# A Fourier mixer on one Trainium2 core: the transform along the features moves from the data to the projection's weights

## The chip, the cores and the metric

One core of a Trainium2 chip runs the whole program. The metric is device time in microseconds (us), from one launch to its end. Engines are called as the profile calls them: PE (matrix multiplies), DVE (vector), ACT (activations, casts), POOL (GpSimd), SP (issues most DMAs). All numbers are fp32; a matmul operand is split in a high part that PE multiplies exactly and a low rest, and a product takes three matmuls (high·high, high·low, low·high).

## The reference

Two sequences, s (512 tokens) and p (1,024 tokens), of 1,024 features go through two layers. The first layer's mixer is the subject:

```python
def fourier_mixer(x, g, w):
    b, s, d = x.shape
    h = rms_norm(x, g).astype(jnp.float32).reshape(b, s, N_FGROUPS, FGROUP_DIM)   # 8 groups of 128
    mixed = jnp.real(jnp.fft.fft2(h, axes=(1, 3), norm="ortho"))
    return mixed.reshape(b, s, d).astype(x.dtype) @ w

# layer 0: x = x + fourier_mixer(x, norm_mix[0], fourier_w)
# layer 1: x = x + attention_mixer(...)
# after each: x = x + (silu(h @ w_gate) * (h @ w_up)) @ w_down     with h = rms_norm(x, norm_ffn[i])
```

The real part of the two-dimensional transform is (cosine along tokens)·(cosine along features) minus (sine)·(sine). All of it is linear, so the transform along the features can be applied to `h` or, transposed, to the rows of `w`.

## The kernel before, in words

Tokens are handled in blocks of 512 columns: one for s, two for p. The program runs in this order.

1. The mixer of s (`lead()`, which runs `mixer("s")`), alone. Rows of tokens are loaded (`load_rows`), squared and summed on ACT (`stats_rows`), and `rsqrt` makes the row scales `r_s` on DVE. Rows are folded along the tokens (`combine`: ACT scales, DVE adds, ACT and DVE split). For each of the 8 feature groups, PE multiplies by the token cosines and sines `mat_s` (`spectra`; a group costs 15 matmuls of 256 or 258 columns and 3 with the fixed row), ACT and DVE split the result into `sd`, and after two groups `features` multiplies by the feature cosines and sines `dd`. Its result is split into `eo`. Beside it the projection's weights of columns 0 to 3 are loaded and folded (`folded`: two POOL sums of 512 columns, an ACT cast, a POOL subtraction of 1,024 columns).
2. The projection of s (`mixer_projection("s")`): 8 column blocks n, each 25 matmuls `eo`·`w` of 256 or 258 columns (one of them with `w64`, the rows that the fold leaves over), then four to five DVE additions to the residual `acc` and a sum of squares. Weights 4 to 7 are folded while it runs; four steps of p's mixer are issued ahead of it.
3. The feed-forward of s, `ffn(0, 0)`: 22 chunks `fc`, each of 72 matmuls of 512 columns (gate and up into two PSUM banks `g`; ACT's silu, the product on DVE (L758) and the split `mid`; then down into `c`, added to `acc` on DVE, L728). A weave issues it together with p's mixer and projection (`aux_0`), by estimated costs of both. Here p's `spectra` and `features` run per group on 128x256 pieces. The result goes to DRAM (`du`), and `spectra_back` loads it again and splits it. The projection of p then loads and folds all 8 weights once more (`folded` with tag `wX`), 50 matmuls for each.
4. The other feed-forwards, woven with attention and its projections. The diff does not touch them.

Every engine takes its instructions in the order in which they were placed, and the tile framework's scheduler chose that order; `pinned` keeps a place. Buffers are shared by tag: `g` has two PSUM banks, `c` (F) two, and `a` one pair of banks.

Of the kernel before, what the change touches and what calls it, by code (L numbers as in the profile page):

```python
# [59 lines left out]
def dft_constants():  # L60
# [31 lines left out]
    i = np.arange(P)  # L92
    ang = 2 * np.pi / P * ((i[:, None] * np.arange(64)[None, :]) % P)
    cos, sin = np.cos(ang), np.sin(ang)
    cos[:, 0] = 0.5
    full = np.zeros((5, P, 192))
    full[0, :, 64:128], full[1, :, 64:128] = split_host(cos)
    full[2, :, 64:128], full[3, :, 64:128] = split_host(sin)
    full[4, :, 64] = (-1.0) ** i

    alt = np.zeros((P, 112))
    alt[:, [8, 40, 72]] = full[4, :, 64:65]
    out["dft_d"] = np.concatenate([full.transpose(1, 0, 2).reshape(P, -1), alt], axis=1).astype(np.float32)
# [20 lines left out]
def trunk_kernel(ctx: ExitStack, tc: tile.TileContext, t: dict):  # L124
# [95 lines left out]
    g_mix0, g_mix1 = gains[:, 0:8], gains[:, 8:16]  # L220
    g_ffn = (gains[:, 16:24], gains[:, 24:32])
    g_q, g_k = gains[:, 32:33], gains[:, 33:34]
    rqc = cp.tile([P, 12, NH], F32, name="rqc")
# [3 lines left out]
    du = dram.tile([P, 2, 4, 514], F32, name="du")  # L227
# [75 lines left out]
    def in_rows(y, temp=None):  # L303

        r = bank()
# [72 lines left out]

    def load_rows(seq):
        if seq == "p":  # L380
            x = h_slot("x_p", F32, "A")[:, 0 : 8 * D].rearrange("p (c n) -> p c n", c=8)
            xs = [x[:, c] for c in range(8)]
        else:
            halves = [w_tile2(2, D) for _ in range(2)]
            xs = [halves[c // 2][:, c % 2] for c in range(4)]
# [4 lines left out]
    def stats_rows(seq, n):  # L390
# [3 lines left out]
        xs = whole[seq]  # L394
        for c in range(n):
            raw = raw_tile(D)
            pinned(act.activation(raw, xs[c], AF.Square, accum_out=s[:, c : c + 1]))
        yield 1.0
        rsqrt(r, s, 1.0 / D, bank()[:, 0 : 4 * n])
        return xs, r  # L400
# [8 lines left out]
    def mixer(seq, done):  # L409
# [4 lines left out]
        rows, r = yield from stats_rows(seq, n)  # L414
# [13 lines left out]
        u = None if two else eo_tile(258, "B")  # L428
        r_ps = None if two else tl("c", [TB], F32, "cX", pools["psX"])

        def alternating(o, x):

            for g in range(NC):
                for b in range(2):
                    v = x(g, b)
                    if v is not None:
                        k = 8 - g % 2 * 4 - g // 2
                        pe.matmul(o, alt[:, k : k + 96], v, start=g == 0 and b == 0, stop=g == NC - 1 and b == 1)

        spec = mpt.tile([P, 2, 2, NC, 2], F32R, name=f"spec_{seq}")  # L440
        ncomb = 2 if two else 1

        def half(v, k):
            return v[:, k * 256 : (k + 1) * 256]

        def combine(q, c):

            def x(k):
                return half(rows[k], q)

            comb = w_tile(ncomb, 2, 2, 256) if two else tl("comb", [ncomb, 2, 2, 256], F32R, ("wF", "rawF")[c])
            fa, fb = (bank(), bank()) if two else (lambda v: (v[:, 0], v[:, 1]))(bank2())
            fs = tmp() if two else None
            for i in range(npair):
                ca, cb = 4 * i + c, 4 * i + 2 + c
                dst = fb if i == npair - 1 else fs
                act.activation(half(fa, i), x(ca), AF.Copy, scale=r[:, ca : ca + 1])
                for k, w in enumerate(scal(cb)):
                    ins = dve.scalar_tensor_tensor(half(dst, k), x(cb), w, half(fa, i), op0=ALU.mult, op1=ALU.add)
                    if two and q == 1 and c == 0:  # L460
                        pinned(ins)
            if not two:
                split(comb[:, 0, :, 0], comb[:, 0, :, 1], fb.rearrange("p (k n) -> p k n", k=2))
                return comb
            for k in range(2):
                e = tmp()
                ops = (ALU.add, ALU.subtract)
                dve.tensor_tensor(half(e, 0), half(fs, k), half(fb, k), op=ops[k])
                dve.tensor_tensor(half(e, 1), half(fs, k), half(fb, k), op=ops[1 - k])
                if k == 1 and c == 0:  # L470
                    xb = tmp(256)
                    dve.tensor_scalar(xb[0:1], x(2)[0:1], r[0:1, 2:3], None, op0=ALU.mult)
                    dve.scalar_tensor_tensor(
                        e[0:1, 256:512], x(6)[0:1], neg[0:1, 6:7], xb[0:1], op0=ALU.mult, op1=ALU.add
                    )
                split(comb[:, k, :, 0], comb[:, k, :, 1], e.rearrange("p (k n) -> p k n", k=2), eng=pool)
            return comb

        def fixed_row(q):

            xr = tmp(256)
            if two:
                xb = tmp(256)
# [836 lines left out]
```

## Time and profile before

| | us |
|---|---|
| median of 3 runs | 3119.56 (3114.71 to 3119.58) |
| the profiled execution, its own time | 3117.2 |
| its span in the trace | 3115.4 |
| PE busy | 3024.0 (97%) |
| DVE, ACT, POOL busy | 1630.1, 1240.3, 1334.4 |

The span leaves 1.8 us of the execution's own time outside. PE is busy in 97% of the span, and its granted clock is 0.9 or more in all but the first of 40 slices; a busy PE at half clock still counts as busy, so both must be read together.

### The profile page before, as it was taken

Reading aid. Unit: us, or ns where it says so; the run is one execution under the profiler, and the core shown is the slowest. Engines: PE = TensorE matmul, PEld = TensorE weight load, DVE = VectorE, ACT = ScalarE, POOL = GpSimd, SP = SyncE. Lnnn points to the kernel's source line nnn. Section 1 sums busy time; section 2 is a strip of 40 time slices with the busy share of each in tenths; the row PEclk is TensorE's granted clock in tenths of the full one; section 3 lists DMA queues with packets and bytes.
Section 4 is the critical chain, followed back from the end, with each engine's and each line's share of the span. In section 5 each row is a group of like instructions: output and inputs, shape, how many; then the busy total and the mean of one; then the engine's idle time right before and its main releaser. Section 6 shows DMA issues by size and latency. Waiting matters only on the chain. (4 is left out here: it accounts for less than half of the span.)

```text
span 3115.4 us, 37725 instructions
## 1 busy us (share of the span) xinstructions
PE 3024.0 (97%) x14554; PEld 2492.2 (80%) x14554; DVE 1630.1 (52%) x2888; ACT 1240.3 (40%) x1806; POOL 1334.4 (43%) x624
## 2 busy tenths in 40 slices
PE   8799999999999999999999999999999999999999
PEld 7787888888887778888878788888787787777777
DVE  4763454454366553353455466656337555655556
ACT  5443232333366632233334477767324222222221
POOL 3645454434333454443343322221546644554452
PEclk7999999999999999999999999999999999999999
DMA  5224553333233554343343311211645411111111
GB/s 192 77 79 131 166 180 101 119 105 99 82 90 99 171 169 132 125 132 103 104 150 98 105 58 57 66 60 51 208 139 189 175 54 55 48 54 49 53 48 61
DMA packets 127927, 329.83 MB, mean 106 GB/s; under 512 B 15314, under 2 KB 23506, under 8 KB 127236
## 3 DMA queue, kind: packets, MB, share of 16 engines
q1 hardware_dynamic: 126164, 318.49, 32.1%
q10 hardware_dynamic: 1296, 4.75, 0.4%
q0 software_dynamic: 288, 4.19, 0.4%
q8 instruction: 114, 1.87, 0.2%
q14 instruction: 65, 0.53, 0.1%
HBM read 282.28 MB, written 45.10 MB: 105 GB/s over the span
## 5 line engine op out<-in xcount | busy, mean ns | idle before, releaser
L277 POOL TENSOR_TENSOR w<-raw,w 128x1024 fp32r<-128x1024 f32 x346 | 826.7, 2399 | 1234.2 <-ACT w L276 1200.1
L728 DVE TENSOR_TENSOR acc<-c,acc 128x512 f32<-128x512 f32 x704 | 482.8, 688 | 479.2 <-PE c L247 475.7
L276 ACT CAST w<-raw 128x1024 fp32r<-128x1024 f32 x346 | 362.2, 1048 | 490.3 <-PE c L247 263.4
L245 PE MATMUL g<-h,w 128*128 128x512 f32 x1408 | 555.2, 394 | 1.3 <-ACT h L238 1.1
L246 PE MATMUL g<-h,w 128*128 128x512 f32 x1408 | 551.5, 392 | 0.6 <-POOL h L239 0.6
L247 PE MATMUL g<-h,w 128*128 128x512 f32 x1408 | 551.2, 392 | 0.0
L245 PE MATMUL c<-mid,w 128*128 128x512 f32 x1056 | 417.4, 397 | 11.3 <-DVE acc L728 6.7
L246 PE MATMUL c<-mid,w 128*128 128x512 f32 x1056 | 414.3, 392 | 3.7 <-DVE mid L239 3.7
L247 PE MATMUL c<-mid,w 128*128 128x512 f32 x1056 | 413.7, 392 | 0.0
L239 POOL TENSOR_TENSOR w<-raw,w 128x1024 fp32r<-128x1024 f32 (+1 forms) x101 | 228.2, 2266 | 340.2 <-ACT w L238 319.1
L838 DVE TENSOR_TENSOR acc<-c,acc 128x512 f32<-128x512 f32 x352 | 240.5, 689 | 191.2 <-PE c L247 190.6
L247 PEld LDWEIGHTS g<-h,w 128*128 128x128 f32 x1408 | 265.0, 188 | 54.7 <-POOL w L277 0.3
L245 PEld LDWEIGHTS g<-h,w 128*128 128x128 f32 x1408 | 265.0, 188 | 53.2 <-ACT h L238 1.3
L246 PEld LDWEIGHTS g<-h,w 128*128 128x128 f32 x1408 | 265.1, 188 | 52.8 <-POOL h L239 1.3
L245 PEld LDWEIGHTS c<-mid,w 128*128 128x128 f32 x1056 | 198.1, 188 | 72.7 <-DVE acc L728 16.6
L246 PEld LDWEIGHTS c<-mid,w 128*128 128x128 f32 x1056 | 198.8, 188 | 43.8 <-DVE mid L239 5.7
L247 PEld LDWEIGHTS c<-mid,w 128*128 128x128 f32 x1056 | 198.6, 188 | 40.3
L246 PE MATMUL c<-h,w 128*128 128x512 f32 x480 | 188.1, 392 | 3.2 <-POOL h L239 3.0
L245 PE MATMUL c<-h,w 128*128 128x512 f32 x480 | 189.2, 395 | 0.0
L247 PE MATMUL c<-h,w 128*128 128x512 f32 x480 | 187.0, 390 | 0.0
L238 ACT CAST w<-raw 128x1024 fp32r<-128x1024 f32 (+1 forms) x101 | 100.2, 1000 | 202.1 <-PE a L247 86.6
L1050 DVE TENSOR_REDUCE col<-a 128x1 f32<-128x1024 f32 (+1 forms) x96 | 100.3, 1045 | 129.2 <-PE a L247 128.9
(305 smaller groups left out, 4996.7 us busy)
## 6 DMA issues: line engine op xcount, KB each, us to landing
raw<-in_down_dram SPq DMA_DIRECT2D x110, 512.0 KB, 3.5
raw<-in_gate_dram SPq DMA_DIRECT2D x88, 512.0 KB, 3.5
raw<-in_up_dram SPq DMA_DIRECT2D x88, 512.0 KB, 3.6
raw<-in_qkv_dram SPq DMA_DIRECT2D x36, 512.0 KB, 3.5
t<-xres SPq DMA_DIRECT2D x56, 256.0 KB, 3.9
raw<-in_wo_dram SPq DMA_DIRECT2D x24, 512.0 KB, 3.4
raw<-in_gate_dram SPq DMA_DIRECT2D x44, 256.0 KB, 2.6
raw<-in_up_dram SPq DMA_DIRECT2D x44, 256.0 KB, 2.9
```

The lines of the kernel that those rows point to most:

```text
L238: act.copy(hi, src)
L239: eng.tensor_tensor(lo, src, hi.bitcast(F32), op=ALU.subtract)
L245: pe.matmul(out, lh, rh, start=first, stop=False)
L246: pe.matmul(out, lh, rl, start=False, stop=False)
L247: pe.matmul(out, ll, rh, start=False, stop=last)
L276: pinned(act.copy(flat[:, 0], raw)) if early else act.copy(flat[:, 0], raw)
L277: pool.tensor_tensor(flat[:, 1], raw, flat[:, 0].bitcast(F32), op=ALU.subtract)
L728: dve.tensor_tensor(acc[dc], ps, acc[dc], op=ALU.add)
L838: dve.tensor_tensor(acc, ps, acc, op=ALU.add)
L1050: dve.tensor_reduce(st[:, 0:1], s_in, op=ALU.max, axis=AX.X)
```

## The change

The feature transform and the feature fold move to the weights and to the rows.

- Weights: `turned_weights` loads the 8 pieces of the projection's matrix (64 folded rows of two groups, 512 columns each), sums and subtracts them (DVE and POOL), splits them, multiplies by the feature cosines and sines with PE, and splits the products into `turned` (used by s straight from SBUF). It writes the unsplit products to DRAM (`cwd`), from where p's projection loads them as plain weights. It runs inside s's mixer, one piece for each step.
- Rows: `prepared` multiplies each row chunk by the gain (in PSUM as rows, `in_rows(gx)`) and folds it along the features: four DVE operations of 128x512 for a chunk of 128 tokens (4 chunks in s, 8 in p). `mixer` then transforms along the tokens only, in `along`, for four pairs of groups: half as many matmuls. Results are split straight into `eo` for p also (`spread`). `du` and `spectra_back` are gone.
- Constants come by POOL's DMAs without a staging tile. One step of p's mixer is issued ahead of s's projection instead of four. The weave's cost for p's part is 105 instead of 140 (times `SLACK`).

```diff
-    def stats_rows(seq, n):
+    def prepared(seq, n, ga, gb, sums):
...
+        for c, x in enumerate(whole[seq]):
+            sq = raw_tile(D) if seq == "p" else bank2().rearrange("p k n -> p (k n)")
+            pinned(act.activation(sq, x, AF.Square, accum_out=s[:, c : c + 1]))
+            y = tl("c", [TB], F32, "cX", pools["psX"])
+            f = sums[c]
+            dve.tensor_tensor(f[:, 0], ga, x[:, 0:TB], op=ALU.mult)
+            dve.tensor_tensor(y, gb, x[:, TB:D], op=ALU.mult)
+            dve.tensor_tensor(f[:, 1], f[:, 0], y, op=ALU.subtract)
+            dve.tensor_tensor(f[:, 0], y, f[:, 0], op=ALU.add)
+            yield 1.0
         rsqrt(r, s, 1.0 / D, bank()[:, 0 : 4 * n])
...
+        def along(k, o, lhs, row):
+
+            for (i, off, w), ps in zip(outs[k], o):
+                extra = k == 0 and i == 0
+                for c in range(2):
+                    m = mat[c][:, :, off : off + w]
+                    mm3(ps[:, 0:w], lhs(c, 0, i), lhs(c, 1, i), m[:, 0], m[:, 1], c == 0, c == 1 and not extra)
...
-    def spectra_back(done):
...
+    def turned_weights(w64, dd, odd, alt):
...
+        def operand(n):
+            raw = raws.pop(0)
+            f = tl("f", [2, TB], F32, "rawF")
+            pinned(dve.tensor_tensor(f[:, 0], raw[:, 0], raw[:, 1], op=ALU.add))
+            pool.tensor_tensor(f[:, 1], raw[:, 0], raw[:, 1], op=ALU.subtract)
+            w = acc_tile("wm", [2, 2, TB], F32R)
+            pinned(act.copy(w[:, 0], f))
+            pool.tensor_tensor(w[:, 1], f, w[:, 0].bitcast(F32), op=ALU.subtract)
...
+        def product(n):
...
+            for k in range(2):
+                ps = bankg()
+                mm3(ps, dd[:, 2 * k], dd[:, 2 * k + 1], w[:, 0, k], w[:, 1, k], True, k == 1)
+                if k == 0:
+                    pe.matmul(ps, alt[0:96, j], w64[0:96, h * TB : (h + 1) * TB], start=False, stop=True)
+                    for b in range(2):
+                        pe.matmul(od[0:96], odd[:, 8 - j : 104 - j], w[:, b, 0], start=j == 0 and b == 0, stop=j == 3 and b == 1)
+                split(wt[:, 0, k], wt[:, 1, k], ps)
+                c = tl("t", [TB], F32, "tX")
+                if k == 0:
+                    act.copy(c, ps)
+                else:
+                    dve.tensor_copy(c, ps)
+                sp.dma_start(cwd[h][:, :, k, j, :], c.rearrange("p (n c) -> p n c", n=4))
...
             if two:
-                w, _ = folded(n, "wX")
+                for m in range(len(ws), min(n + 2, NC)):
+                    ws.append(weights(cwd[m // 4][:, m % 4].rearrange("p k j c -> p (k j c)")))
...
     def lead():
-        m = mixer("s", got_s)
+        ws = turned_weights(w64, dd, odd, alt)
+        next(ws)
+        stacked(w64[0:96], stage[0:96], 64)
+        m = mixer("s", got_s, u_s, xrs_s, zz_s)
         for k, v in enumerate(m):
             yield v
...
+            if k in (1, 3) or k >= 5:
+                next(ws, None)
...
-    for _ in range(4):
+    for _ in range(1):
         next(x_0)
     weave(follow(), 1.0)
-    weave(ffn(0, 0, lambda: first["h"]), FFN_US, x_0, (80.0 + 60.0) * SLACK)
+    weave(ffn(0, 0, lambda: first["h"]), FFN_US, x_0, (45.0 + 60.0) * SLACK)
```

The order of instructions shows three places. The first is DVE at the start of s's mixer. Before, `rsqrt` follows at once on the casts of the constants, and its last step, the row scales `r_s`, leads straight to the mask, the fixed row and the first folds; `x_139` holds rows, `m_252` a masked scale.

```order
L291 SCALAR_TENSOR_TENSOR r_s<-c_238,col_239 128x4
L405 TENSOR_TENSOR m_252<-r_s,mask 128x1
L421 TENSOR_SCALAR neg_s<-r_s 128x4
L487 TENSOR_SCALAR t_284<-x_139,r_s 1x256
L406 TENSOR_SCALAR m_252<-m_252 128x1
L487 TENSOR_SCALAR t_382<-x_139,r_s 1x256
L459 SCALAR_TENSOR_TENSOR a_261<-x_139,m_252,a_261 128x256
L239 TENSOR_TENSOR xrs_286<-t_284,xrs_286 1x256
L459 SCALAR_TENSOR_TENSOR a_261<-x_139,m_252,a_261 128x256
```

In the changed kernel these stand ahead of `rsqrt` (`x_140`, `x_141` are the rows, `x_249`, `x_250` the folded sums, `c_159` and `c_172` the gain, `stage_152` the leftover rows of the weights, `f_267` a folded piece of them).

```order
L406 TENSOR_TENSOR x_250<-c_159,x_141 128x512
L407 TENSOR_TENSOR c_255<-c_172,x_140 128x512
L611 TENSOR_TENSOR eo_150<-stage_152,eo_150 32x1024
L408 TENSOR_TENSOR x_249<-x_249,c_255 128x512
L407 TENSOR_TENSOR c_262<-c_172,x_140 128x512
L409 TENSOR_TENSOR x_249<-c_255,x_249 128x512
L408 TENSOR_TENSOR x_249<-x_249,c_262 128x512
L407 TENSOR_TENSOR c_277<-c_172,x_141 128x512
L409 TENSOR_TENSOR x_249<-c_262,x_249 128x512
L631 TENSOR_TENSOR f_267<-raw_243 128x512
L408 TENSOR_TENSOR x_250<-x_250,c_277 128x512
```

So 16 operations of `prepared`, the split L611 and two folds L631 stand where none stood; two splits of the first turned weight (L241 of `w_326`) stand around the end of `rsqrt`, and the row scales come after the first of them.

The second place is DVE at the start of `ffn(0, 0)`. Before, the product with silu for chunk 0 (L758, on `g_1213`) comes after the last row of `normed` (L345), p's splits and three folds of 128x256:

```order
L345 SCALAR_TENSOR_TENSOR t_1208<-acc_788,gains,c_1166 128x512
L242 SCALAR_TENSOR_TENSOR sd_1234<-a_1236,gains,sd_1234 128x2x128 x2
L242 SCALAR_TENSOR_TENSOR spec_p<-a_1236,gains,spec_p 128x2
L242 SCALAR_TENSOR_TENSOR sd_1235<-a_1258,gains,sd_1235 128x2x128 x2
L242 SCALAR_TENSOR_TENSOR spec_p<-a_1258,gains,spec_p 128x2
L459 SCALAR_TENSOR_TENSOR t_1316<-x_p_690,m_735,c_1314 128x256 x2
L459 SCALAR_TENSOR_TENSOR c_1315<-x_p_690,m_738,c_1314 128x256
L758 TENSOR_TENSOR g_1213<-g_1213,t_1419 128x512
```

In the changed kernel, 25 operations of `prepared` for p (L406 to L409) stand between the last row of `normed` (now L347) and the same product, now L785 on `g_1093`. The last two of them and what follows, up to the split of `mid_1224`:

```order
L409 TENSOR_TENSOR x_p_682<-c_1209,x_p_682 128x512
L407 TENSOR_TENSOR c_1216<-a_1109,x_p_682 128x512
L785 TENSOR_TENSOR g_1093<-g_1093,t_1221 128x512
L408 TENSOR_TENSOR x_p_682<-x_p_682,c_1216 128x512
L406 TENSOR_TENSOR x_p_682<-a_1109,x_p_682 128x512
L409 TENSOR_TENSOR x_p_682<-c_1216,x_p_682 128x512
L241 TENSOR_TENSOR mid_1224<-g_1093,mid_1224 128x512
```

So the split of chunk 0's `mid` is the 30th operation behind the last L347; before it came after few and shorter ones.

The third place is PE at the same point in the changed kernel. After chunk 0's gate and up (48 matmuls into the two banks of `g_1093`) come chunk 1's gate into `g_1242` (24) and its up into `g_1243`, which takes the bank that `mid_1224` has to be read from first; here is the end of that and the first `c<-mid` of chunk 0:

```order
L248 MATMUL g_1243<-h_1059,w_1234 128x512
L249 MATMUL g_1243<-h_1059,w_1234 128x512
L247 MATMUL g_1243<-h_1059,w_1234 128x512
L248 MATMUL g_1243<-h_1059,w_1234 128x512
L247 MATMUL c_1283<-mid_1224,w_962 128x512
L247 MATMUL c_1315<-mid_1224,w_962 128x512
L249 MATMUL g_1243<-h_1059,w_1234 128x512
L248 MATMUL c_1283<-mid_1224,w_962 128x512
L249 MATMUL c_1283<-mid_1224,w_962 128x512
```

No matmul of p stands ahead of or among these rows after the start of `ffn(0, 0)`, where before p's `a<-mat_p` did; in the changed kernel p's first one stands some 300 rows later.

## Rows read from the trace of the kernel before

**Rows 1.** Of the profile's page, its parts 1 and 2: busy time by engine; then PE's granted clock in 40 slices of the span.

```profile
PE 3024.0 (97%) x14554; PEld 2492.2 (80%) x14554; DVE 1630.1 (52%) x2888; ACT 1240.3 (40%) x1806; POOL 1334.4 (43%) x624
...
PEclk7999999999999999999999999999999999999999
```

**Rows 2.** Windows of PE by stage: the mixer of s; its projection; three stretches inside `ffn(0, 0)` with p's mixer (to about 300 us) and p's projection. Columns: stretch, its length, PE busy (instructions), granted clock (1.00 is 2.4 GHz, 0.50 is 1.2 GHz), DMA share, GB/s.

```profile
18.00:73.70 55.70, 46.77 (x207) 0.66 0.51 180
73.70:110.90 37.20, 27.86 (x200) 0.86 0.33 104
132.00:200.00 68.00, 65.46 (x358) 1.00 0.25 78
200.00:285.00 85.00, 84.10 (x444) 1.00 0.34 104
285.00:345.00 60.00, 51.06 (x260) 0.91 0.51 156
```

**Rows 3.** PE's waits: what waits <- what it waits for, us in total, times, longest. The first row is of 0 to 76 us, the others of 73.7 to 122.6 us.

```profile
PE g L245 <- ACT comb L238: 8.1, 5, 2.3
...
PE g L245 <- DVE acc L695: 6.7, 1, 6.7
...
PE g L247 <- POOL w L636: 1.0, 1, 1.0
```

**Rows 4.** The same inside `ffn(0, 0)`: two rows of 118 to 200 us, one of 200 to 300 us, two of 300 to 400 us.

```profile
PE c L246 <- DVE mid L239: 2.5, 1, 2.5
PE a L245 <- DVE spec_p L242: 1.5, 1, 1.5
...
PE c L245 <- ACT mid L238: 2.6, 1, 2.6
...
PE c L247 <- POOL w L636: 8.0, 6, 2.3
PE c L245 <- ACT w L635: 1.4, 1, 1.4
```

**Rows 5.** PE's timeline, three pairs of neighbours: start in us, duration, instruction. The distance of the two starts is what one costs in a dense run: of 256 columns at full clock, of 258 at half, of 512 at full.

```profile
104.17 0.28 PE L245 MATMUL c<-eo,w 128*128 128x256 f32 x1
104.29 0.28 PE L246 MATMUL c<-eo,w 128*128 128x256 f32 x1
...
308.07 0.42 PE L245 MATMUL c<-eo,w 128*128 128x258 f32 x1
308.29 0.42 PE L246 MATMUL c<-eo,w 128*128 128x258 f32 x1
...
500.34 0.39 PE L245 MATMUL g<-h,w 128*128 128x512 f32 x1
500.56 0.39 PE L246 MATMUL g<-h,w 128*128 128x512 f32 x1
```

**Rows 6.** PE's groups of instructions from 116 to 300 us, p's transforms: count (x), then busy us and mean ns of one.

```profile
L245 PE MATMUL a<-mat_p,w 128*128 128x258 f32 (+1 forms) x64 | 19.5, 305 | 2.4 <-DVE spec_p L242 2.4
...
L533 PE MATMUL c<-sd,dd 128*128 128x256 f32 x128 | 17.3, 285 | 0.0
```

**Rows 7.** Three moments of the start, as in a timeline (start, duration in us): ACT when the last half of s's rows has landed, DVE's row scales, PE's first matmul of the projection of s.

```profile
11.26 1.06 ACT L397 ACTIVATE raw<-x 128x1024 f32<-128x1024 f32 x1 [1.48 <-DMA x<-in_rows_s_dram]
...
16.80 0.16 DVE L291 SCALAR_TENSOR_TENSOR r_s<-c,col 128x4 f32<-128x4 f32 x1
...
73.67 0.39 PE L245 MATMUL c<-eo,w 128*128 128x258 f32 x1 [0.26 <-ACT eo L238]
```

**Rows 8.** DVE's groups from 0 to 300 us (count, busy us, mean ns of one): a split of 128x512, one of 128x256, and one operation on a single row of 256, at a time when POOL works beside it (L472) and when it does not (L487).

```profile
L239 DVE TENSOR_TENSOR comb<-a,comb 128x512 fp32r<-128x512 f32 x8 | 5.5, 692 | 4.7 <-ACT comb L238 4.5
...
L239 DVE TENSOR_TENSOR eo<-c,eo 128x256 fp32r<-128x256 f32 x8 | 3.3, 421 | 0.5 <-ACT eo L238 0.3
...
L472 DVE TENSOR_SCALAR t<-x_p,r_p 1x256 f32<-1x256 f32 x4 | 3.5, 871 | 0.0
...
L487 DVE TENSOR_SCALAR t<-x,r_s 1x256 f32<-1x256 f32 x4 | 1.3, 334 | 0.0
```

**Rows 9.** The timeline at 86 us, of POOL and of DVE.

```profile
85.97 4.72 POOL L636 TENSOR_TENSOR w<-raw,w 128x1024 fp32r<-128x1024 f32 x2 [1.16 <-ACT w L635]
...
86.37 2.07 DVE L405 TENSOR_TENSOR m<-r_p,mask 128x1 f32<-128x1 f32 x2
88.36 2.36 DVE L421 TENSOR_SCALAR neg_p<-r_p 128x8 f32<-128x8 f32 x1
```

**Rows 10.** POOL's groups from 0 to 120 us: a subtraction of 128x1024 and a sum of 128x512.

```profile
L636 POOL TENSOR_TENSOR w<-raw,w 128x1024 fp32r<-128x1024 f32 x8 | 18.9, 2374 | 10.8 <-ACT w L635 10.7
...
L629 POOL TENSOR_TENSOR raw<-raw 128x512 f32<-128x512 f32 x8 | 10.2, 1277 | 48.8 <-DMA raw<-in_wf_dram 41.5 <-PE g L247 7.0
```

**Rows 11.** The start of `ffn(0, 0)`: PE's first matmul of it; on DVE the last row of `normed` and the split of chunk 0's `mid`.

```profile
122.60 0.73 PE L245 MATMUL g<-h,w 128*128 128x512 f32 x2 [1.07 <-ACT h L238]
...
128.96 0.75 DVE L345 SCALAR_TENSOR_TENSOR t<-acc,gains,c 128x512 f32<-128x512 f32 x1 [0.51 <-POOL h L239]
...
146.26 0.67 DVE L239 TENSOR_TENSOR mid<-g,mid 128x512 fp32r<-128x512 f32 x1
```

**Rows 12.** The DMA view from 0 to 130 us: the mean rate and, in 40 slices of that stretch, the rate.

```profile
DMA packets 5820, 19.67 MB, mean 151 GB/s; under 512 B 1050, under 2 KB 1050, under 8 KB 5556
...
GB/s 79 370 435 266 0 0 91 415 303 0 161 0 18 146 5 180 359 421 343 159 184 115 275 299 275 9 156 5 0 57 105 5 3 169 154 137 190 39 122 0
```

More of the change, by code (lines that the diff above doesn't have):

```diff
@@ L413, in mixer @@
         mat, rowm = mats[seq], rows_m[seq]
-        rows, r = yield from stats_rows(seq, n)
+        if two:
+            g2 = bank2()
+            ga, gb = in_rows(gx[:, 0:4], ps=g2[:, 0]), in_rows(gx[:, 4:8], ps=g2[:, 1])
+            sums = [x.rearrange("p (k n) -> p k n", k=2) for x in whole[seq]]
+        else:
+            ga, gb = done["gain"]
+            sums = [h[:, i] for h in (tl("x", [2, 2, TB], F32, "wX") for _ in range(2)) for i in range(2)]
+        r = yield from prepared(seq, n, ga, gb, sums)
         yield 1.0
@@ L426, in scal @@
             return r[:, c : c + 1], neg[:, c : c + 1]
[L428 to L466, printed above, removed]
@@ L527, in along @@
-        def along(o, kind, x, first, last):
-            for par in range(2):
-                cols = slice(64 - 64 * par, 192 - 64 * par)
-                terms = ((4, 0), (4, 1)) if kind == 1 else ((kind, 0), (kind, 1), (kind + 1, 0))
-                for n, (a, b) in enumerate(terms):
-                    pe.matmul(
-                        o, dd[:, a, cols], x(par, b), start=first and par == 0 and n == 0,
-                        stop=last and par == 1 and n == len(terms) - 1,
-                    )
@@ L538, in features @@
[L538 to L556 removed]
+                    xb = tmp()
@@ L596, in mixer @@
-        done["u"], done["r64"] = u, r64
-        yield 0.3
+        r64 = mpt.tile([P, 516], F32R, tag="r64", name=f"r64_{seq}")
+        second = []
+        if two:
+            ends_folded()
+            for c in range(2):
+                second.append(unit(1, c))
+                yield 1.0
+            u = h_slot("eo", F32R, "A")[:, 0 : 16 * 516].rearrange("p (h k c n) -> p h k c n", h=2, k=2, c=4)
+        for j in range(NC // 2):
+            js = slice(j * P, (j + 1) * P)
+            if two:
+                a2 = bank2()
+                o = [a2[:, 0], a2[:, 1]]
+            else:
+                o = [bank()]
+            along(0, o, lambda c, b, i: combs[c][:, b, i, js], [x[0:1, js] for x in xrs])
+            if two:
+                spread(u, 0, j, o)
+            else:
+                split(u[:, 0, 0, j, 0:258], u[:, 1, 0, j, 0:258], o[0][:, 0:258])
+            yield 2.2 if two else 0.5
+            if j < 2 and not two:
+                second.append(unit(1, j))
@@ new lines, in mixer @@
+        if not two:
+            ends_folded()
+        for j in range(NC // 2):
+            js = slice(j * P, (j + 1) * P)
+            if two:
+                a2 = bank2()
+                o = [a2[:, 0], a2[:, 1]]
+            else:
+                o = [bank()]
+            along(1, o, lambda c, b, i: second[c][:, b, i, js], None)
+            if two:
+                spread(u, 1, j, o)
+            else:
+                split(u[:, 0, 1, j, 0:256], u[:, 1, 1, j, 0:256], o[0][:, 0:256])
+            yield 1.5 if two else 0.5
```

402 lines of the change are left out of this document (194 added, 208 removed).

## The prediction

> **What bounds the kernel now.** I read the busy shares and the granted clock first. PE is busy for 97% of the span and its clock is high in all but the first slice [rows 1]; what PE no longer has to do is therefore gained in full, wherever PE is the engine that the others wait for. The windows by stage say where that is so. In s's mixer PE shows 46.8 of 55.7 us busy, but at a mean clock of 0.66: half of that stretch is waiting and PE running at 1.2 GHz because it waits. In s's projection it is 27.9 of 37.2 us at 0.86. Inside `ffn(0, 0)`, where p's mixer runs, PE is busy 65.5 of 68 and 84.1 of 85 us at full clock, and it drops to 51.1 of 60 at 0.91 where p's projection sets in [rows 2]. So `ffn(0, 0)` is bound by PE, the two stages ahead of it by chains of other engines. The waits name these: in s's mixer ACT's half of a split; in the projection one DVE addition of 6.7 us and POOL's weight [rows 3]; in p's projection POOL's weights, 8.0 us in six waits [rows 4].
>
> The price of a matmul is the distance of two starts: 0.12 us for 256 columns at full clock, 0.22 at half clock, 0.22 for 512 at full clock [rows 5]. All stages are costed apart below, against the profiled execution's own 3117.2 us.
>
> **s's mixer, now 18 to 73.7 us.** By the diff the transform goes from 184 large matmuls to 69 of some 258 columns and 72 of 512 (the weights'), 22.1 us before and 8.3 + 15.8 = 24.1 us after at full clock: nothing gained for PE as such. PE waited there, so the stage ends where another engine ends, and that is now DVE. Its row scales were ready at 16.8 us. In the changed kernel 16 operations of `prepared`, L611 and two L631 stand ahead. The second half of the rows has landed by 11.3 us [rows 7]; from there 19 operations of 0.69 us [rows 8] end at 24.4, `rsqrt` (12 small ones, at about 0.2 each by the 0.16 us of its last one [rows 7]) and one split bring r_s to about 28 us. Behind it the order has 38 more operations of 0.69, nine of 0.42 and 2.5 us of small ones: 32.5 us, so DVE's floor is 60.5. To this I add collisions with POOL. Beside a POOL subtraction of 4.72 us two tiny DVE operations took 2.07 us (for a pair) and 2.36 us [rows 9]; another one-row operation took 0.87 us beside POOL and 0.33 without [rows 8]. The changed order has 15 operations of such kinds in this stretch (L631 with two inputs in SBUF, small ones with one scalar) while POOL works through 8 pieces of 1.28 + 2.37 = 3.65 us [rows 10]. At the 0.54 us between the two one-row groups that makes 8 us; at 0 it makes none, at about 2 us each (rows 9) 30. I take 0.54, since most of the fifteen meet POOL only at times: DVE ends at 68.5, the first matmul of the projection starts at about 69. That is **-4.7**, with bounds -13 and +16. PE running at half clock throughout would need 48 us from r_s on and end at 76, which lies inside these bounds.
>
> A rule of the Trainium skill speaks against the change at this place. SBUF — State Buffer, Who interferes with whom, says that a DVE operation with two SBUF inputs, or a copy or tensor_scalar in its two-port mode, shuts out a GpSimd operation that reads SBUF and is shut out by it for that one's whole length. The trace agrees in kind, since 128x1 operations took over 1 us there [rows 9]. By the rule alone, with each of the fifteen held for a whole POOL operation of 2.37 us, DVE would end at 96 and the sum below would come out 27 us later.
>
> **s's projection, now 73.7 to 110.9 us.** Its matmuls stay. 200 of them at 0.12 are 24.0 us. The 6.7 us wait for an addition came from DVE, which had the operations on p beside POOL in between [rows 9]; now one step of p instead of four is issued ahead, so it goes. The weights' wait of 1.0 goes, since `turned` lies ready in SBUF [rows 3]. Of the 13 us over the dense 24.0, 7.7 us go by name and some 2 of the clock with them, because PE fell to 0.86 around these waits: **-10**, bounds -12 (all but a start at half clock) and -5 (the wait stays in part, since `odds` and the POOL work of the last piece may still be late). The 11.7 us from its end to the first matmul of `ffn(0, 0)` at 122.6 [rows 11] are `rsqrt` and `normed`, the same before and after: 0. So `ffn(0, 0)` begins at about 108.
>
> **p inside ffn(0, 0).** Here PE is the bound, so matmuls count in full. p's transforms were 192 with `mat_p`, 24 with the fixed row and 128 with `dd` (the counts are the program's; [rows 6] show 128 with `dd` and 64 of the three with `mat_p`): 344 at 0.12 = 41.3 us. They become 123 (14.8 us) and 8 fp32 ones of 128 columns for the gain. No row prices these; between 0.06 us (their columns by rows 5) and 0.39 (a whole one of 512 columns there) I take 0.26, since exact fp32 has to cost more than the single pass: 2.1 us, and **-24.4** in all. In p's projection POOL's two sums go, and of 2 x 1.28 + 2.37 = 4.9 us for one weight 2.4 stay [rows 10]; then PE's waits for `w`, 8.0 and 1.4 us, and the 2.6 for `mid` [rows 4] go: **-12**. With them goes the half clock around 285 to 345 us, (1 - 0.91) x 60 = 5.4 us [rows 2]: **-5**.
>
> Against that stands the start. With t = 0 at the first matmul of `ffn(0, 0)`, L345 ended at 7.1 us before (129.7 - 122.6) and the split of chunk 0's `mid` at 24.3 [rows 11], and PE had p's matmuls to run meanwhile, so it waited 2.5 + 1.5 us only [rows 4]. In the changed order the split is the 30th operation behind the last L347: 7.1 + 30 x 0.69 = 27.8. PE runs 48 + 24 matmuls of 512 columns, 16.3 us, and then has nothing of p to fill with until the bank is free. The stall is 27.8 - 16.3 = 11.5 us where 4 were: **+7**, and **+2** for a clock that falls after so long a wait, as it did around the waits of rows 2 (some ten matmuls at 0.22 more). Later, p's units also split 128x512 pieces on DVE, between PE and PE's next chunk; eight of them each late by one operation of 0.69 are **+6**, bounds 0 and 15 (two late each, and the rest of `prepared`). Together: -24.4 - 12 - 5 + 7 + 2 + 6 = **-26**, bounds -41 and -15.
>
> **The sum.** -4.7 - 10 - 26 = -41 us, 3076 for the profiled execution. The median of the runs stands 2.4 us above that one (3119.6 to 3117.2), so I say **3078**.
>
> **The rivals.** *More gain:* DVE meets POOL hardly at all and the start has no stall, because p's first matmuls come in earlier or PE finds the bank free. Lead -13, projection -12, ffn -41 (no term of the start and of later units): -66, or 3054. For it speaks that small operations took 0.33 us without POOL [rows 8]; against it, that the order fixes 30 operations ahead of the split. *A long lead:* DVE and POOL block each other at 2 us each time, lead +16, projection -8, ffn -15 with the same blocking in p: -7, or 3113; at half that price it would be about 3098. Rows 9 speak for it, and POOL is busy for 29 us of this stage; against it, that most of the fifteen are not beside a POOL operation of 4.7 us. The truth could be anywhere between this and the forecast. *Slower, by DMA:* `cwd` writes 4.2 MB more before `ffn(0, 0)` can have its weights. Before, 19.67 MB moved in 130 us, at 151 GB/s [rows 12]; I count about 23 MB that must have moved before that point. At 151 GB/s this takes 152 us instead of 122.6, +30, which is what the ffn gives back (-26) and so the point from which it decides; at 130 GB/s, if small pieces slow the queue, 177 us, or 3148. Against it: the same view has slices of 359 to 435 GB/s with nothing in others [rows 12], so the queue is idle for lack of issue, and 4.2 MB at 359 are 12 us. In a sentence by itself: the Trainium skill, DMA: Bandwidth & Descriptors, Specifications, holds pieces of 512 bytes or more to run at full rate, by which nothing would be lost; no row here shows such a write. *No change* would need PE not to have been the bound in `ffn(0, 0)`, against 84.1 of 85 us busy [rows 2].
>
> **How the numbers follow.** The forecast 0.60 (3062 to 3096), more gain 0.18 (down to 3045), the long lead 0.12 (3098 to 3115, a third of it within 0.2% of before), no change 0.04, slower 0.06. 0.2% or 6 us is what a measurement of this kernel tells from no change. The range leaves out some 0.06 below 3050, which is under the full gain, and 0.13 above 3110, the dearest part of the long lead and what lies beyond. Faster 0.86, same 0.08, slower 0.06.
>
> **What would show it.** Right: r_s at about 28 us on DVE instead of 16.8; the first matmul of the projection near 69; in the projection no wait for an addition above 2 us; in `ffn(0, 0)` a PE wait of 8 to 12 us for `mid` 16 us after its start, no waits for POOL's `w`, and the stage shorter by 26 us. L631 and the small operations of DVE at means above 1 us would speak for the long lead. Wrong would make it above all a wait of PE for `turned` in the projection, ACT (which casts in both the weights' and the rows' chain, and squares rows after L609) as the bound of the lead, or DMA gaps in front of the first gate weights.

## The result and the profile after

The changed kernel takes 3079.94 us (median of 4 runs, 3077.77 to 3081.78) beside 3118.82 us of the kernel before (3114.71 to 3119.58): a ratio of 0.9878, 95% interval 0.9861 to 0.9895. The prediction was 3078 us, and 3050 to 3110. The total is right; two of its terms are wrong by 15 and 13 us, in opposite directions.

The first view gives the windows of PE of the changed kernel by stage, to be read beside [rows 2]: the mixer of s, its projection, and two stretches at the start of `ffn(0, 0)`. Columns as there.

```profile
18.00:84.30 66.30, 45.91 (x187) 0.79 0.63 203
84.30:108.50 24.20, 24.20 (x201) 1.00 0.41 141
118.90:145.00 26.10, 21.98 (x86) 0.93 0.28 99
145.00:200.00 55.00, 49.00 (x204) 0.97 0.27 86
```

The lead is longer than before (66.3 us after 55.7) and still runs at a clock of 0.79; the projection is now dense, 24.2 of 24.2 us busy at full clock where it was 27.9 of 37.2 (in the control, which came out of the lead at half clock, 26.0). Four moments in the changed kernel's timeline (start, duration): the row scales, the first matmul of the projection, the first matmul of `ffn(0, 0)`, and the product with silu of chunk 22, its last:

```profile
28.52 0.16 DVE L293 SCALAR_TENSOR_TENSOR r_s<-c,col 128x4 f32<-128x4 f32 x1
...
84.28 0.38 PE L247 MATMUL c<-eo,w 128*128 128x258 f32 x1
...
118.88 0.50 PE L247 MATMUL g<-h,w 128*128 128x512 f32 x1
...
561.72 0.70 DVE L785 TENSOR_TENSOR g<-g,t 128x512 f32<-128x512 f32 x1 [1.41 <-PE g L249]
```

The last of these stood here in the kernel before; the others are in [rows 7, 11].

```profile
604.63 0.70 DVE L758 TENSOR_TENSOR g<-g,t 128x512 f32<-128x512 f32 x1 [1.40 <-PE g L247]
```

So the stages compare like this. "After" is the profiled execution of the changed kernel (span 3076.0 us).

| stretch | before, us | after, us | difference | predicted |
|---|---|---|---|---|
| start to first matmul of the projection | 73.7 | 84.3 | +10.6 | -4.7 |
| projection of s | 37.2 | 24.2 | -13.0 | -10 |
| its end to the first matmul of `ffn(0, 0)` | 11.7 | 10.4 | -1.3 | 0 |
| `ffn(0, 0)`, to the product of chunk 22 | 482.0 | 442.8 | -39.2 | -26 |
| the rest, which the diff does not touch | 2510.8 | 2514.3 | +3.5 | 0 |

The sum is -39.4. The rest scatters: in a second profile of the same changed kernel (the control below) it was 2510.7 us, and the mixer's end stood at 86.2. Over these two profiles and those of e3, e4 and e4x, which have the same lead, that end lies between 84.3 and 87.9 us; so a single stage is known to some 2 to 4 us. `ffn(0, 0)` is the steadiest: 442.8 and 443.1 us in the two profiles.

**Where the lead went.** PE's waits in the lead (18 to 84.3 us):

```profile
PE c L652 <- POOL wm L635: 9.5, 3, 7.3
PE g L248 <- POOL wm L635: 4.1, 3, 1.8
PE g L247 <- DVE t L658: 2.5, 1, 2.5
```

PE now waits for POOL's low part of a piece of weights, once for 7.3 us. The chain of that wait is seen on three engines: SP's issues, POOL's sum of piece 2, PE.

```profile
17.13 2.41 SPq L393 DMA_DIRECT2D x_p<-in_rows_p_dram  x3
21.47 0.33 SPq L620 DMA_DIRECT2D raw<-in_wf_dram  x1
...
31.19 1.26 POOL L632 TENSOR_TENSOR f<-raw 128x512 f32<-128x512 f32 x1 [6.20 <-DMA raw<-in_wf_dram]
...
34.80 0.74 PE L652 MATMUL c<-wm,eo 128*96 128x512 f32 x1 [7.27 <-POOL wm L635]
35.34 0.63 PE L247 MATMUL g<-wm,eo 128*128 128x512 f32 x1
35.77 0.63 PE L248 MATMUL g<-wm,eo 128*128 128x512 f32 x1
```

Three of p's four SP loads stand in SP's queue ahead of piece 2 (issued at 21.5 us), and ACT's queue has four more; piece 2 has landed only when POOL has waited 6.2 us for it, at 31.2. PE comes out of its 7.3 us with starts 0.43 us apart for 512 columns, twice the price in [rows 5]: half clock. The DMA view from 0 to 90 us (busy tenths of the 16 DMA engines in 40 slices of 2.25 us; then KB of one transfer, median us from issue to landing) shows what else is moved:

```profile
DMA  0899999499999991006406449108627048999999
...
DMA packets 13050, 20.74 MB, mean 230 GB/s; under 512 B 1081, under 2 KB 9216, under 8 KB 12662
...
raw<-in_wf_dram SPq DMA_DIRECT2D x8, 512.0 KB, 5.9
cwd<-t SPq DMA_DIRECT2D x16, 256.0 KB, 3.1
```

The 256 KB writes of `cwd`, in pieces of 512 bytes, landed after 3.1 us; they are not what is slow. The rival by DMA, weights that come late for `ffn(0, 0)`, did not come true: the mean is 230 GB/s, and PE waits for no weight at its start. But from 18 to 34 us the engines were 90% busy or more. In that stretch p's 4 MB went over them together with piece 2, which took 9.7 us from its issue to POOL's sum (3.6 us in e8, where p's rows come later). DVE, which I had taken for the bound of this stage, waited for ACT's casts (18 to 84 us; count, busy us, mean ns, idle time before):

```profile
L241 DVE TENSOR_TENSOR w<-g,w 128x512 fp32r<-128x512 f32 x16 | 10.9, 687 | 10.7 <-ACT w L240 10.7
L631 DVE TENSOR_TENSOR f<-raw 128x512 f32<-128x512 f32 x8 | 8.0, 1006 | 0.0
...
L241 DVE TENSOR_TENSOR comb<-a,comb 128x512 fp32r<-128x512 f32 x4 | 2.7, 684 | 7.3 <-ACT comb L240 7.3
...
L496 DVE TENSOR_SCALAR col<-x,r_s 128x8 f32<-128x8 f32 x2 | 2.5, 1284 | 0.0
L241 DVE TENSOR_TENSOR zs_s<-t,zs_s 128x288 fp32r<-128x288 f32 x1 | 2.4, 2405 | 0.3 <-ACT zs_s L240 0.3
```

The collisions with POOL are there: L631 has a mean of 1.006 us instead of the 0.68 of a dense run, L496 1.28 us for 128x8 (0.22 for one of the two in e6), and the split of `zs_s` 2.4 us where one of 128x258 takes 0.41. With three small L505 of 0.59 us (0.22 for three others of that line) they add up to some 8 us, as I had put down. But DVE stood idle for 18 us in front of two groups alone, so its sum of work set no end.

**Where ffn(0, 0) won more.** PE's busy time in the whole stretch, first in the changed kernel, then in the one before:

```profile
118.90:561.72 442.82, 429.89 (x2109) 0.99 0.38 123
```

```profile
122.60:604.63 482.03, 462.41 (x2331) 0.98 0.39 122
```

PE's idle time fell from 19.6 to 12.9 us, and the clock from a loss of about 9.6 (0.02 of 482) to 4.4 us (0.01 of 443). These two are -12, the clock's part of it uncertain by a few us because the clock is given to 0.01; the rest, -27, is work that PE no longer has. PE's waits there that are left, of 110 to 200 us and of 200 to 600 us:

```profile
PE g L247 <- ACT t L784: 4.5, 3, 2.7
PE c L247 <- DVE acc L755: 3.6, 2, 1.8
...
PE a L247 <- DVE ss L333: 1.5, 1, 1.5
PE c L249 <- POOL w L279: 1.4, 1, 1.4
```

At the start, where I had put a stall of 11.5 us, PE waited 2.7 and 0.8 us:

```profile
133.81 0.60 PE L247 MATMUL g<-h,w 128*128 128x512 f32 x1 [2.74 <-ACT t L784]
...
141.91 0.50 PE L247 MATMUL g<-h,w 128*128 128x512 f32 x1 [0.75 <-ACT t L784]
...
140.84 0.69 DVE L785 TENSOR_TENSOR g<-g,t 128x512 f32<-128x512 f32 x1
...
141.26 0.60 ACT L784 ACTIVATE t<-g 128x512 f32<-128x512 f32 x1 [4.58 <-PE g L249]
...
143.31 0.69 DVE L241 TENSOR_TENSOR mid<-g,mid 128x512 fp32r<-128x512 f32 x1
```

`g_1243`, chunk 1's up, starts at 141.91, ahead of the split of `mid`, L241 at 143.3, which still reads chunk 0's product. So it does not take the bank of that product, as I had said where I described the change. It starts 0.05 us after ACT's silu of chunk 1 has ended (L784, at 141.26), which the profile names as what it waited for: it takes the bank of chunk 1's own gate, which this silu has just read. The first wait of 2.7 us is for chunk 0's silu, which had a square of p's rows (L403) and a table load of 1.28 us ahead of it on ACT. PE also came to `g_1243` later than by my count: 141.2 us is 22 us after the start of the feed-forward, not 16, since it had waited 0.6 us for `h` and 2.7 for silu and had then run some nine matmuls at half clock.

### The profile page after: what moved, and what is told of

The parts are those of the page before. It is cut to its first block, busy times and chain, and to the rows that moved or that the text cites. A ratio compares the mean times of both kernels' runs of the same rounds, so it can differ in the third digit from the quotient of the medians.

```text
span 3076.0 us, 36978 instructions
## 1 busy us (share of the span) xinstructions
PE 2985.8 (97%) x14268; PEld 2448.0 (80%) x14268; DVE 1642.7 (53%) x2863; ACT 1219.5 (40%) x1749; POOL 1279.8 (42%) x583
## 4 chain that ended last, share of the span: by engine, by line
PE 83%; POOL 5%; DVE 4%; DMA 3%; issue 3%; ACT 2%; SPq 0%; POOLq 0%; ACTq 0%; DVEq 0%
PE c L247 12%; PE c L248 12%; PE c L249 12%; PE g L249 10%; PE g L247 10%; PE g L248 10%; PE a L247 4%; PE a L249 4%; PE a L248 4%; PE c L1095 2%; POOL w L279 2%; POOL w L241 1%; DVE col L1078 1%; POOL h L241 1%; PE c L1028 1%
## 5 line engine op out<-in xcount | busy, mean ns | idle before, releaser
L279 POOL TENSOR_TENSOR w<-raw,w 128x1024 fp32r<-128x1024 f32 x354 | 846.1, 2400 | 1316.3 <-ACT w L278 1249.6
L278 ACT CAST w<-raw 128x1024 fp32r<-128x1024 f32 x354 | 370.8, 1049 | 530.7 <-PE c L249 281.3
L241 POOL TENSOR_TENSOR w<-raw,w 128x1024 fp32r<-128x1024 f32 (+1 forms) x101 | 228.3, 2268 | 337.5 <-ACT w L240 316.4
L247 PEld LDWEIGHTS c<-mid,w 128*128 128x128 f32 x1056 | 197.8, 188 | 73.7 <-DVE acc L755 20.3
```

Of the source, the lines that this page charges most:

```text
L241: eng.tensor_tensor(lo, src, hi.bitcast(F32), op=ALU.subtract)
L247: pe.matmul(out, lh, rh, start=first, stop=False)
L278: pinned(act.copy(flat[:, 0], raw)) if early else act.copy(flat[:, 0], raw)
L279: pool.tensor_tensor(flat[:, 1], raw, flat[:, 0].bitcast(F32), op=ALU.subtract)
```

## The experiments

All differences in us are to a control, the changed kernel itself, run with e1 to e3. The runs were made in four groups, and the kernel before, run in each, had medians of 3117.2 us (control to e3), 3116.2 (e4 to e8), 3113.8 (e9 to e11) and 3118.5 (e12); a difference in us from one group to another carries these few us, a ratio does not. Each ratio to the kernel before has an interval of about 0.0015 on either side (5 us), so that steps of 4 to 7 us rest on the range of the runs and on the trace together.

**c_after**, no edit.

> The changed kernel itself, as a control for the runs beside it: all theories expect 3080 us (3078 to 3082), 0.988 of the kernel before.

Measured: 3079.02 us (3077.42 to 3081.47), ratio 0.9879 (0.9864 to 0.9894).

**e1_p_rows_late.** The loads wait for a one-element copy from the first turned weight.

```diff
         for c, x in enumerate(xs):
+            if seq == "p": after(x, turned[0][:, 0, 0])
             (sp if c % 2 == 0 else act).dma_start(x, t[f"rows_{seq}"][:, c, :])
```

> The loads of p's rows wait until the first turned weight is split (about 29 us), so that pieces 2 and 3 of the projection's weights are no longer queued behind 4 MB. Theory 'late pieces' (s's mixer took until 84.3 us because POOL waited 6.2 us for piece 2 and PE then 7.3 us for POOL): the first matmul of the projection comes at 77 to 78 us and the time is 3073 to 3074 us. Theory 'loop' (each piece costs one round of cast, subtraction, products and split of some 6 us, whenever it arrives): piece 2 comes earlier, but the end moves by 0 to 2 us, 3078 to 3080.

Measured: 3082.75 us (3080.05 to 3086.04), 0.9891 (0.9876 to 0.9906). Neither theory's time. The trace (PE's wait from 60 to 110 us; POOL's sum of piece 2; SP's issues; the first matmul of the projection):

```profile
PE c L247 <- DVE acc L718: 5.6, 1, 5.6
...
25.62 1.28 POOL L632 TENSOR_TENSOR f<-raw 128x512 f32<-128x512 f32 x1 [0.18 <-DMA raw<-in_wf_dram]
...
70.84 0.33 SPq L393 DMA_DIRECT2D x_p<-in_rows_p_dram  x1
...
80.38 0.58 PE L247 MATMUL c<-eo,w 128*128 128x258 f32 x1
```

Piece 2 is there 5.6 us earlier, and the projection starts at 80.4 us instead of 84.3 to 87.9. But SP now issued p's loads at 71 to 84 us, in front of the residual of s, and PE waited 5.6 us for an addition to it. The gain was given back at once; the experiment shows the price of late pieces in the lead, not in the time.

**e2_warm.**

```diff
                 ps = bankg()
+                for _ in range(4 if k else 10):
+                    pe.matmul(ps[:, 0:P], ones, ones, start=True, stop=True)
                 mm3(ps, dd[:, 2 * k], ...)
```

> PE multiplies ones ahead of each turned product (10 fillers of 128 columns ahead of a piece's first half, 4 ahead of its second, into the bank that the product then starts anew), so that it does not idle there. Theory 'clock' (the lead is long because PE runs it at half clock, 0.79 on the mean): granted clock above 0.9 in the lead, the projection starts 5 to 8 us earlier, time 3072 to 3075 us. Theory 'loop' with POOL and ACT as the slow links: the clock rises and the end stays, 3079 to 3081; with fillers in the way up to 3086.

Measured: 3074.62 us (3071.14 to 3078.76), 0.9863 (0.9846 to 0.9879). The ranges of this and the control overlap. PE's window from 40 to 84 us:

```profile
40.00:84.00 44.00, 44.00 (x312) 1.00 0.65 195
...
81.41 0.28 PE L247 MATMUL g<-eo,w 128*128 128x258 f32 x1
```

PE is never idle, fillers included, and the clock is full, and still the projection starts at 81.4 us, only 3 to 6 us earlier. The fillers also stand ahead of the products, so that this is what clock and fillers bring together, not the price of the clock alone.

**e3_matmuls_back.** In p's part of `along`, ahead of each of 16 groups:

```diff
+                for _ in range(14):
+                    pe.matmul(ps[:, 0:w], lhs(0, 0, i), mat[0][:, 0, off : off + w], start=True, stop=True)
                 for c in range(2):
```

> 224 matmuls of 256 or 258 columns are put back into p's transform, as fillers ahead of each of its 16 groups, as many as the change took out (221), with no other work of the old kernel. Theory of the prediction (PE is the bound in the first feed-forward, each matmul counts in full): 224 x 0.12 = +27 us, 3107 (3104 to 3109). Rival (the gain came from waits and the clock, and PE has slack now): less than +14 us, under 3094.

Measured: 3103.82 us (3100.91 to 3105.72), 0.9957 (0.9942 to 0.9972): +24.8 us for 224 matmuls, 0.11 each; in the trace `ffn(0, 0)` takes 470.6 us to the product of chunk 22, 27.8 more than before the edit, 0.12 each. PE's matmuls count in full or nearly so, as predicted.

**e4_sums_back.** In p's weights, behind the load:

```diff
         sp.dma_start(raw, src)
+        for o in (ALU.add, ALU.subtract):
+            pool.tensor_tensor(raw[:, 0:TB], raw[:, 0:TB], raw[:, TB:D], op=o)
```

> Of the old weight chain of p's projection, POOL's two sums of 512 columns are put back ahead of the cast (one adds, the other takes away again, so that the weights stay the same but for rounding); nothing else changes. Theory of the prediction (the waits for w, 9.4 us, and the half clock around them, 5 us, were due to the sums): +10 to +14 us, 3089 to 3093. Rival (the 32 to 40 us that POOL gains per projection are covered by PE, since the weave hands weights out early enough): 0 to +3 us.

Measured: 3089.81 us (3087.84 to 3091.86), 0.9918 (0.9901 to 0.9935): +10.8 us, the size that was expected. But in the trace `ffn(0, 0)` is only some 7 us longer (449.9 us to the product of chunk 22); the other 4 lie in stages that the edit does not touch. And the wait stands elsewhere:

```profile
270.07 0.58 PE L247 MATMUL a<-eo,w 128*128 128x256 f32 x1 [5.98 <-DVE ss L333]
...
269.00 0.42 DVE L717 TENSOR_TENSOR t<-c,t 128x256 f32<-128x256 f32 x1 [6.75 <-DMA t<-in_xT_dram]
```

PE has one wait of 6.0 us for a bank (1.6 in the control), because DVE waited 6.8 us for a load of the residual. No wait names `w` for more than 1.4 us. The projection of p has little slack for POOL's sums; that it was POOL's subtraction itself that PE waited for, as in [rows 4], is not what this run repeats.

**e4x_spread.** In `prepared`:

```diff
-            yield 1.0
+            yield 1.0 if seq == "s" else 4.0
```

> The steps of p's `prepared` get a cost of 4.0 instead of 1.0 in the weave, so that only some 7 instead of 25 DVE operations stand ahead of the product of chunk 0. Theory 'start' (these operations hold the bank that PE waits for at the start of the feed-forward): the waits of 2.7 and 0.8 us go and the half clock behind them, -3 to -5 us, 3074 to 3076. Rival (the stall only moves to where p's mixer begins later): 3078 to 3082.

Measured: 3072.51 us (3070.67 to 3074.24), 0.9862 (0.9845 to 0.9879): -6.5 us, the ranges apart. PE's wait for silu from 110 to 200 us, where the control has 4.5 in three:

```profile
PE g L247 <- ACT t L784: 1.3, 1, 1.3
```

The product of chunk 0 came 13.5 us after the start of the feed-forward instead of 22.0, and the stage to the product of chunk 22 took 434.3 us, 8.5 to 8.8 less. So the steps of `prepared` ahead of that product did cost something, about half of what I had priced for the start and the later units (15 us). The edit moves whole steps, a square on ACT and four DVE operations each; the waits that went are for ACT's silu, and which of the two engines' work delayed it the run does not tell apart.

**e6_no_copies.**

```diff
-                c = tl("t", [TB], F32, "tX")
-                if k == 0:
-                    act.copy(c, ps)
-                else:
-                    dve.tensor_copy(c, ps)
+                c = wt[:, 0, k].bitcast(F32)
```

> The 16 copies of the unsplit products (ACT 8, DVE 8, 128x512 each) are left out: the high halves alone are written to DRAM, as many bytes, so that p's projection uses weights without their low part. Theory 'loop' (a product's bank is held by cast, subtraction and copy, so each piece costs ACT, DVE and PE one round after the other): the round gets 0.6 to 1.3 us shorter, the projection of s starts 5 to 10 us earlier, time 3070 to 3075. Theory 'late pieces' or 'clock': the copies lie beside the wait, 0 to -2 us, 3077 to 3080.

Measured: 3074.11 us (3070.16 to 3075.47), 0.9863 (0.9843 to 0.9884): -4.9 us.

```profile
71.33 0.39 PE L247 MATMUL c<-eo,w 128*128 128x258 f32 x1
...
PE c L247 <- DVE acc L718: 5.0, 1, 5.0
```

The lead is 13 us shorter or more, with p's rows still ahead of the pieces; 5.0 us go to a wait for the residual, which could not be loaded as early. The copies, 16 times 0.6 to 0.7 us on ACT and DVE, are the larger of the two parts of the lead that I could take away. By which way they act is not shown: they hold PE's two banks, but PE's only wait for one of them in the changed kernel was 2.5 us (L658 above); they also stand in ACT's and DVE's queues, and POOL's waits for ACT's cast of a piece (L634) fell from 24.1 us in the lead to 16.1 (but to 16.2 in e8 too, which keeps the copies).

**e8_rows_mid.** `load_rows("p")` is called in `lead()` at its step 7 instead of in `aux_0`, with the copy of e1.

> p's rows are loaded between 35 and 60 us, behind pieces 2 and 3 and ahead of the residual of s, which e1 had put behind them (its 5.6 us wait of PE for an addition). If late pieces cost the 4 to 6 us of the lead that e1's trace showed, and the loss in the projection was the collision: projection from 79 to 81 us, no wait for an addition above 1 us, time 3073 to 3076. If e1's gain in the lead was only the clock's scatter: 3078 to 3082.

Measured: 3071.67 us (3068.37 to 3074.08), 0.9859 (0.9841 to 0.9877): -7.4 us, the ranges apart.

```profile
25.20 1.29 POOL L632 TENSOR_TENSOR f<-raw 128x512 f32<-128x512 f32 x1
...
74.53 0.39 PE L247 MATMUL c<-eo,w 128*128 128x258 f32 x1
...
110.82 0.50 PE L247 MATMUL g<-h,w 128*128 128x512 f32 x1
```

POOL no longer waits for piece 2, the projection starts at 74.5 us, the feed-forward at 110.8 us (118.9 and 122.5 in the two profiles of the changed kernel), and PE waits for an addition for 1.4 us at most. This is more than expected, and what e1 had been meant to show.

**e9_rows_and_spread**, e8 and e4x together.

> p's rows loaded in the middle of the lead (as e8) and p's `prepared` spread in the weave (as e4x) together. If the two are apart in cause (weights' pieces in the lead; the bank at the start of the feed-forward), their gains of 7 to 8 and 6 to 7 us add: 3064 to 3067 us. If both are the same gain twice (an earlier start only makes p's work meet the same chunks): 3070 to 3072.

Measured: 3061.92 us (3061.05 to 3064.56), 0.9835 (0.9822 to 0.9849): -17.1 us, of which some 3 are the faster group; by the ratios it is -13.7 us, beside -11.5 for e8 and e4x together. The trace has both gains, the feed-forward's start at 112.7 us (110.8 in e8) and 433.8 us for the stage to the product of chunk 22 (434.3 in e4x). The causes are apart.

**e10_split_through**, on e9: both halves of a turned weight are written, and p's projection loads them as they are.

```diff
+                for b in range(2):
+                    sp.dma_start(cwd[h][:, :, b, k, j, :], wt[:, b, k].bitcast(F32).rearrange("p (n c) -> p n c", n=4))
...
-                    ws.append(weights(cwd[m // 4][:, m % 4]...))
+                    ws.append(w_tile(2, NC, P)); pool.dma_start(ws[-1]..., cwd[m // 4][:, m % 4]...)
```

> As e9, and the turned weights go to DRAM as the two split halves (twice the bytes), from where p's projection loads them as they are: no 16 copies in the lead, no cast and no POOL subtraction in p's projection. Theory 'loop' (the copies hold the product's bank, as e6 showed): the projection starts at 66 to 70 us, time 3054 to 3061. Theory 'DMA' (32 writes of 256 KB in SP's queue hold back the pieces and the residual behind them): the lead stays above 74 us or the additions wait, 3064 to 3072.

Measured: 3066.59 us (3063.41 to 3070.41), 0.9851 (0.9838 to 0.9864): 4.7 us more than e9, though the projection started at 70.8 us instead of 76.7. It is the time of theory 'DMA', by its second condition:

```profile
60.25 19.73 SPq L655 DMA_DIRECT2D cwd<-w  x16
80.08 2.13 SPq L698 DMA_DIRECT2D acc<-in_xT_dram  x4
...
PE c L247 <- DVE acc L718: 7.4, 1, 7.4
...
40.00:75.00 35.00, 28.62 (x134) 0.85 1.06 354
```

The last sixteen writes kept SP for 19.7 us, the residual was issued at 80.1 us, and PE waited 7.4 us for an addition. From 40 to 75 us the 16 DMA engines were full.

**e11_and_warm**, e9 with 6 and 2 fillers.

> As e9, with 6 and 2 fillers ahead of the turned products as in e2. Theory 'clock' (half clock in the lead is a cause of its own): 3 to 4 us less than e9. Theory 'loop': with the pieces in time PE waits less, so that the fillers are in the way: 0 to +2 us against e9.

Measured: 3068.67 us (3065.53 to 3070.93), 0.9855 (0.9842 to 0.9868): 6.7 us more than e9, the ranges apart, and the projection starts at 80.3 us. With the pieces in time the fillers do not pay, and cost more than I had allowed. Theory 'clock' is not borne out; how much of the half clock in the lead is only a consequence of the waits is not shown, since the fillers bring their own time with the clock.

**e12_residual_by_act**, on e10:

```diff
-                sp.dma_start(xs[-1], t["xT"][b][:, n, :])
+                (sp if two else act).dma_start(xs[-1], t["xT"][b][:, n, :])
```

> As e10, and the eight loads of s's residual are issued from ACT's queue instead of SP's, where 16 writes of the turned weights (19.7 us in e10's trace) stood ahead of them. Theory 'SP queue' (e10 lost in the projection what it won in the lead, 7.4 us of PE's wait for an addition, because SP issued the loads late): no wait for an addition above 2 us, the feed-forward begins at 107 to 110 us, 3056 to 3061 us. Theory 'DMA' (the 16 engines are full, 1.06 of their time from 40 to 75 us, so that the loads land late from any queue): 3063 to 3068.

Measured: 3060.50 us (3058.32 to 3068.43), 0.9820 (0.9804 to 0.9837).

```profile
PE c L247 <- DVE acc L718: 1.6, 2, 1.4
...
108.57 0.72 PE L247 MATMUL g<-h,w 128*128 128x512 f32 x2
```

The wait is gone and the feed-forward begins at 108.6 us, with the DMA engines as full as in e10 (1.07 of their time from 40 to 84 us): what counted was the place in SP's queue. The interval lies just below that of e10 and overlaps that of e9. e9 and e12 both beat the kernel before and the changed one.

## Why the prediction was right, and where it was not

**Where PE is the bound.** Right. Matmuls that are put back count at 0.11 to 0.12 us (e3) against 0.12 put down, and the windows that I read as full are the ones that shrank.

**The row scales** at 28 us: 28.5.

**The lead, -4.7: wrong, +10.6.** The failed step is "the stage ends where another engine ends, and that is now DVE". I added up DVE's work behind the row scales and took its end for the end of the stage. The two sizes in it were about right (r_s at 28 us; collisions of some 8 us), but no engine is busy all through: DVE waits for ACT's casts, ACT's queue for PE's products, PE for POOL's low part, POOL for a cast or a piece. A piece goes round these engines with two PSUM banks and two raw pieces. The matmul L650, which comes once for each piece, shows the rounds; here are the first and the last of eight:

```profile
25.61 0.39 PE L650 MATMUL g<-eo 96*128 96x512 f32 x1
...
81.31 0.63 PE L650 MATMUL g<-eo 96*128 96x512 f32 x1
```

That is 8.0 us a round in the mean; it was 6.7 in e6 and 6.8 in e8. What shortens a round or starts it earlier shortens the lead: without the copies 13 us or more (e6), with pieces 2 and 3 in time some 10 (e8). Both were to be read before: p's loads ahead of the pieces in SP's order, and 16 copies that read the banks into which PE multiplies next, on two engines that the next piece has to pass.

**The projection, -10: -13.0.** Both waits went, and so did all of the half clock; the term was 3 us short (1 us in the control, where the first matmuls still ran at half clock).

**ffn(0, 0), -26: -39.2.** The mis-sized term is what I set against the gain, +7, +2 and +6. By the windows above, waits gave -6.7 us where I had +1 in sum (-12 + 7 + 6), the clock some -5 where I had -3, and work some -27 where I had -24.4. The start cost 3.5 us of waits and some 2 of half clock where 4 were before, because chunk 1's up does not take the bank of chunk 0's product, so that PE did not wait there for the split to free a bank; and the later units left waits of 3.6 us for additions and 1.3 for `mid`. Spreading the steps gave back 6.5 us (e4x), less than half of the 15. The term of the matmuls was about right (24.4; 24.8 in e3, 27.8 in its stage). That of POOL's sums with the clock (12 + 5) was too large by e4 (10.8 us, 7 of them in the stage), and e4 does not show that the sums act by the wait that I named.

**The rivals.** The long lead came near to true in its length (+10.6 us, +12.5 in the control; its price was +16) but not by its mechanism, since DVE and POOL blocked each other for only some 8 us, where it wanted 30. Its rows were misread in one point: the 4.72 us of POOL in [rows 9] are two subtractions (x2) of 2.36 us each. The gain in full nearly came true for `ffn(0, 0)` (-39.2; -41 there). The total is where forecast because these two nearly cancel, which is luck and not insight. By the rule of the Trainium skill (SBUF — State Buffer, Who interferes with whom) all fifteen operations could have been shut out for whole POOL operations; the trace shows it for some (L496 at 1.28 us, L631 at up to 1.78), not for most. The DMA rival fell: 20.7 MB moved in the first 90 us, at 230 GB/s, and no weight was waited for at the start of `ffn(0, 0)`; what DMA did cost, late pieces in the lead, was in none of the terms.

**Still open:** which part of the lead is the loop alone, and by which way the copies act in it. In e12 it ends at 70.5 us with no copies and with pieces 2 and 3 in time, 10 us above DVE's floor of 60.5; PE's waits for POOL's low part are 10.6 us there. The load is itself a link of the round: in e8 and e12 POOL took up each of pieces 2 to 7 within 0.3 us of its landing, 3.5 to 8.9 us after it was issued, and it is issued only when one of the two raw buffers is free. That more raw buffers would shorten the lead, or POOL's subtraction cut in halves, so that PE starts on the first, was not tried.

## What to carry to other kernels

A stage in which each piece passes four engines through two buffers is not priced by the sum of the busiest engine: follow one piece round, count what stands ahead of it in each queue and what holds its buffer, and multiply the round. A transfer that nothing waits for yet (here p's rows) still costs when it is queued ahead of one that is waited for, and moving it must look at what it then stands in front of (e1 against e8). Where a product has to wait for a bank, do not take from the names which of the banks it gets: the trace shows which instruction it waited for.

## What was not expected of the hardware

While the 16 DMA engines were full (1.06 of their time in the window from 40 to 75 us), one write of 256 KB took 1.2 us of SP in the mean (16 in 19.7 us, e10), where one took 0.5 us in the changed kernel (at 41.3 and 46.8 us, with the engines less full); here the full DMA showed as a late issue of what came next in that queue, the residual. And a granted clock of 1.00 instead of 0.7 to 0.8 over 44 us of the lead (e2) moved its end by only 3 to 6 us, fillers included.
